# The mlp of an RWKV/NSA block: loads and weight sums moved ahead at its two seams, 512-column products in the up projection, and an accumulator in seven separate PSUM banks

## The chip, the cores and the metric

One core of one Trainium2 chip runs the whole program. The metric is device time in microseconds (us), the median of three runs. TensorE (PE) multiplies, VectorE (DVE), ScalarE (ACT) and GpSimd (POOL) do the elementwise work, SyncE (SP) issues most of the transfers.

## The reference, cut to what matters

One block for 512 tokens of width 2048; the change touches the lines from `h` on. `D_FF` is 8192.

```python
mixed = jax.nn.sigmoid(gate_a) * (y_a @ w_out_rwkv[l]) + jax.nn.sigmoid(gate_b) * (y_b @ w_out_nsa[l])
h = h + mixed @ w_o[l]
hn = rmsnorm(h, norm_mlp[l])
h = h + jnp.square(jax.nn.relu(hn @ mlp_w_up[l])) @ mlp_w_down[l]
...
return rmsnorm(h, norm_final)
```

## The kernel before

Matrices stay transposed: 128 features on the partitions, the T = 512 tokens along a row. To keep float32 accuracy every factor is split into a high and a low part (type fp32r), and a product is three matmuls into one PSUM accumulator: hi·x_hi, hi·x_lo, lo·x_hi.

**Jobs.** The projections `w_on`, `w_o` and `w_down` are jobs of one queue (`add_job`, L74). A job is one block of 128 output rows: 16 k-tiles, three matmuls each (L100 to L102), in an accumulator `acc`. Weights come in pieces of four k-tiles (`split`, L60: load `wraw` on SP's queue, ACT casts `whi`, DVE subtracts for `wlo`), prefetched two pieces ahead. A job's `evac` reads the accumulator once it is complete.

**The w_o jobs** (`o_evac`, L144) make `h`, store it to `hd` in device memory, and add up its squares on POOL (two operations of each block, L1159 and L1161, for the norm's sum `ssq`). ACT scales `h` into `q`, and of each pair of blocks `factors` (L172) makes one tile `hx`: seven linear combinations of four quarters (two feature blocks by two token halves of H = 256), each in a high and a low part. hx0 to hx5 are made while the jobs run, hx6 and hx7 at the head of `mlp_up`.

**The up projection** (`mlp_up`, L1203) computes 32 column blocks j with a Strassen–Winograd scheme: seven products of quarter size in place of eight, each over two halves of the k-tiles (kh = 0, 1). A product in one half is four k-tiles by three matmuls of 256 columns, so a half is 84 matmuls and a block j 168. `prep` (L1215) makes the weights of a half one half ahead: SP loads 1 MB `raw`, DVE and POOL make the sums s1 and s2 (half of each on either engine), ACT casts `h3` (three plain weights) and `hs` (two sums, twice), DVE subtracts for the low parts `l3` (L1225) and `ls` (L1233). `hs` and `ls` have two buffers each: one for s1 and one for s2, so those of the next half must wait until the products of this half have read them. The accumulator of a block has eight slots of 256 columns in four banks; two accumulators alternate over j, so that the evacuation of one block (`evac`, L1253: one ACT copy, four DVE additions, relu and square on ACT, a store to `ud`) lies beside the products of the next block.

The norm's scale is computed on the way: `rms` and `bcast` are called inside the first half's products, and its square `rb` multiplies the down projection's sum at the end, since relu and square let a positive factor through.

**The down projection** (`mlp_down`, L1296) has four quarters q of 16 jobs. `hidden(j)` (L1305) loads `u` from `ud` and splits it into `xs`. The last quarter runs in two token halves; each of its evacuations multiplies by `rb`, adds `h` (loaded again as `hl`, L1359) and adds up squares for the final norm.

**What sets the order.** PE and POOL run in the order in which the code is written (`manual_schedule`). DVE, ACT and SP are ordered by the compiler's scheduler within what the data allow; buffers (`bufs=`) decide when a tile may be written again. SP's instructions issue in order: one that waits holds up those behind it.

## Time and profile before

| | |
|---|---|
| median of three runs | 3146.84 us (3144.91 to 3146.86) |
| the profiled execution | 3148.25 us, span of its trace 3146.5 us, mean clock 0.99 |
| DVE busy, share of the span | 58% |
| ACT busy, share of the span | 38% |
| POOL busy, share of the span | 20% |

The up projection runs from 1723.7 to about 2372.9 us of the span, the down projection from there to the end. A row of the timeline gives an instruction's start, its duration, engine, line and operation, and in brackets the idle time ahead of it with what ended that. A row of a stretch gives the busy time of each engine, the granted clock of PE (1.00 is the full 2.4 GHz), the share of time in which the DMA engines moved data, and GB/s.

### The profile page before, as it was taken

To read this page: it belongs to the slowest core of one execution; us is meant where nothing else is said; L and a number is where in the kernel's file an instruction comes from. 1 tells how busy PE (TensorE), PEld (TensorE's weight loads), DVE (VectorE), ACT (ScalarE), POOL (GpSimd) and SP (SyncE) were. 2 spreads that over 40 slices of the span, in tenths; PEclk is the share of its full clock that TensorE was granted. 3 is DMA by queue.
4 is the path that set the end of the run, shared out by engine and by line. 5 is a ranking of instruction groups with operands and counts; after the bars stand their busy time and mean duration, and the time that the engine had idled before them with its cause. 6 is when DMAs were issued, how large, how long until landed. Compare 5 with 4: busy or idle time off the path is not lost.

```text
span 3146.5 us, 49636 instructions
## 1 busy us (share of the span) xinstructions
PE 3051.5 (97%) x19296; PEld 2589.6 (82%) x19296; DVE 1824.0 (58%) x3220; ACT 1181.7 (38%) x1999; POOL 644.1 (20%) x673
## 2 busy tenths in 40 slices
PE   9999999999999999999998999999997999999997
PEld 7777777777777878777887999999996888888987
DVE  7855665575553457774455677777774233332665
ACT  4322332233222345554333444444443232222443
POOL 2312222222220000001222333333330000000244
PEclk9999999999999999999999999999998999999999
DMA  4222222222224422125544333333335242342565
GB/s 162 81 87 76 79 79 75 71 81 85 78 77 145 133 92 65 62 90 189 167 147 131 127 132 131 133 131 132 132 118 193 95 148 94 105 137 94 166 198 178
DMA packets 167901, 369.29 MB, mean 117 GB/s; under 512 B 18928, under 2 KB 28656, under 8 KB 159472
## 3 DMA queue, kind: packets, MB, share of 16 engines
q1 hardware_dynamic: 156384, 339.28, 33.1%
q10 hardware_dynamic: 10640, 24.73, 2.1%
q8 instruction: 151, 2.47, 0.3%
q0 software_dynamic: 640, 2.10, 0.2%
q14 instruction: 86, 0.70, 0.1%
HBM read 322.06 MB, written 41.94 MB: 116 GB/s over the span
## 4 chain that ended last, share of the span: by engine, by line
PE 61%; DVE 2%; DMA 1%; ACT 1%; issue 1%; POOL 0%; SPq 0%; DVEq 0%; ACTq 0%; POOLq 0%
PE acc L1247 20%; PE acc L100 12%; PE acc L102 12%; PE acc L101 12%; PE po L1036 1%; PE sc L1003 1%; PE pt L1025 1%; DMA wraw<-w_down 1%; DMA u<-ud 1%; DVE wlo L68 0%; PE sc L947 0%; ACT whi L67 0%; DVE hx L1186 0%; PE po L982 0%; DVE kst L921 0%
## 5 line engine op out<-in xcount | busy, mean ns | idle before, releaser
L68 DVE TENSOR_TENSOR wlo<-wraw,whi 128x512 fp32r<-128x512 f32 x752 | 541.5, 723 | 590.1 <-ACT whi L67 585.2
L67 ACT CAST whi<-wraw 128x512 fp32r<-128x512 f32 x752 | 465.0, 619 | 1090.7 <-PE acc L101 978.5
L100 PE MATMUL acc<-xn,whi 128*128 128x512 f32 x1472 | 611.5, 415 | 1.3 <-DVE th L380 1.3
L102 PE MATMUL acc<-xn,wlo 128*128 128x512 f32 x1472 | 578.4, 393 | 0.0
L101 PE MATMUL acc<-xn,whi 128*128 128x512 f32 x1472 | 577.4, 392 | 0.0
L100 PE MATMUL acc<-xs,whi 128*128 128x512 f32 (+1 forms) x1280 | 450.4, 352 | 21.2 <-ACT xs L925 16.2
L102 PE MATMUL acc<-xs,wlo 128*128 128x512 f32 (+1 forms) x1280 | 449.8, 351 | 1.9 <-DVE wlo L68 1.9
L101 PE MATMUL acc<-xs,whi 128*128 128x512 f32 (+1 forms) x1280 | 449.5, 351 | 2.0 <-DVE xs L926 2.0
L1247 PE MATMUL acc<-hx,hs 128*128 128x256 f32 x2048 | 365.8, 281 | 0.0
L100 PEld LDWEIGHTS acc<-xn,whi 128*128 128x128 f32 x1472 | 278.3, 189 | 60.4 <-issue 6.5
L102 PEld LDWEIGHTS acc<-xn,wlo 128*128 128x128 f32 x1472 | 277.5, 189 | 61.4
L101 PEld LDWEIGHTS acc<-xn,whi 128*128 128x128 f32 x1472 | 278.7, 189 | 46.1
L1247 PEld LDWEIGHTS acc<-hx,hs 128*128 128x128 f32 x2048 | 315.2, 189 | 0.0
L100 PEld LDWEIGHTS acc<-xs,whi 128*128 128x128 f32 x1280 | 241.5, 189 | 58.8 <-ACT xs L925 17.3
L1247 PE MATMUL acc<-hx,ls 128*128 128x256 f32 x1024 | 287.6, 281 | 0.0
L1247 PE MATMUL acc<-hx,h 128*128 128x256 f32 x1536 | 276.9, 282 | 4.7 <-ACT h L1224 4.7
L101 PEld LDWEIGHTS acc<-xs,whi 128*128 128x128 f32 x1280 | 241.5, 189 | 38.8 <-DVE xs L926 3.9
L102 PEld LDWEIGHTS acc<-xs,wlo 128*128 128x128 f32 x1280 | 241.6, 189 | 38.5 <-DVE wlo L68 3.4
L1233 DVE TENSOR_TENSOR ls<-s,hs 128x1024 fp32r<-128x1024 f32 x128 | 181.2, 1416 | 109.1 <-ACT hs L1232 109.1
L1247 PEld LDWEIGHTS acc<-hx,h 128*128 128x128 f32 x1536 | 237.0, 190 | 5.2 <-ACT h L1224 5.2
L1247 PE MATMUL acc<-hx,l 128*128 128x256 f32 x768 | 216.5, 282 | 5.2 <-DVE l L1225 5.2
L1247 PEld LDWEIGHTS acc<-hx,ls 128*128 128x128 f32 x1024 | 193.3, 189 | 0.0
(351 smaller groups left out, 4217.3 us busy)
## 6 DMA issues: line engine op xcount, KB each, us to landing
wraw<-w_down SPq DMA_DIRECT2D x320, 256.0 KB, 3.2
raw<-w_up SPq DMA_DIRECT2D x64, 1024.0 KB, 5.0
wraw<-w_gate SPq DMA_DIRECT2D x128, 256.0 KB, 3.0
wraw<-w_rkv SPq DMA_DIRECT2D x96, 256.0 KB, 3.1
wraw<-w_o SPq DMA_DIRECT2D x64, 256.0 KB, 3.2
ud<-e ACTq DMA_DIRECT2D x32, 512.0 KB, 3.7
u<-ud SPq DMA_DIRECT2D x32, 512.0 KB, 5.3
thd<-th SPq DMA_DIRECT2D x32, 256.0 KB, 3.5
```

The costliest lines, as they stand in the source:

```text
L67: nc.scalar.copy(hi, raw)
L68: lo_eng.tensor_tensor(lo, raw, hi.bitcast(F32), OP.subtract)
L100: nc.tensor.matmul(ps, hi[:, j], xh, start=k == 0, stop=False)
L101: nc.tensor.matmul(ps, hi[:, j], xl, start=False, stop=False)
L102: nc.tensor.matmul(ps, lo[:, j], xh, start=False, stop=last)
L1003: nc.tensor.matmul(ps[:, 0:n], q, self.kst[h][:, x, br, 0:n], start=x == 0, stop=x == 1)
L1025: nc.tensor.transpose(pt[:, b], s[:, 128 * b:128 * b + 128], self.ident)
L1036: nc.tensor.matmul(self.o[j][64 * h:64 * h + 64, 128 * i:128 * i + 128], self.vn[:, b, v0:v0 + 64], pT[h][:, b], start=False, stop=i == 3 ...
L1233: nc.vector.tensor_tensor(l, s, h.bitcast(F32), OP.subtract)
L1247: nc.tensor.matmul(o, w[wi][part][:, 128 * i:128 * i + 128], x[:, xi, xp], start=kh == 0 and i == 0 and m == 0 and slot in opens, stop=kh ...
```

## The change

1. **The last four w_o jobs are cut in two**: first k-tiles 0 to 11 of all four, then the last four k-tiles of each, in four accumulators that stay open (`box`, `close`). Their evacuations are called in `mlp_up`, behind the first `prep`, with the second `prep` behind them. `hx6` and `hx7` lie in a pool `px` that opens where the pool `po` closed.
2. **The norm's sum of squares** goes straight into `self.rb`, and its scale is computed in the first quarter of the down projection.
3. **From j = 2 on the products are "wide"**: hi·[x_hi | x_lo] is one matmul of 512 columns, which leaves the two partial sums side by side in one bank, and lo·x_hi (256 columns) is added to the first of them. Seven products take seven banks: four in accumulator A, three in B, and there is one of each, for all j. The evacuation comes in two parts. `evac_a` reads A after the fourth product of the second half, `evac_b` reads B after the seventh.
4. **At the seam to the down projection** its first loads, the job list and two pieces of weights are written ahead of the last block's `evac_b`.
5. **At the end** the factor `rb` and the load of `hl` go to the third quarter (q = 2), and the squares of the last quarter go from POOL to ACT.

```diff
@@ step / add_job
-            ps = self.acc_pool.tile([128, T], F32, name="acc", bufs=2)
+            if job[4]:
+                ps = job[4].pop()
+            else:
+                ps = self.acc_pool.tile([128, T], F32, name="acc", bufs=self.accs)[:, 0:job[1][0][0].shape[-1]]
...
+            if not close:
+                box.append(ps)
+            else:
+                evac(ps, ld) if load else evac(ps)
@@ mix
-        for m in range(KC):
+        for m in range(KC - 4):
             self.add_job(a["w_o"][m], self.xs, *self.o_evac(m))
-        self.drain(KC)
+        boxes = [[] for m in range(4)]
+        for c, ks in enumerate((slice(0, 12), slice(12, 16))):
+            for m in range(4):
+                evac, load = self.o_evac(KC - 4 + m)
+                self.add_job(a["w_o"][KC - 4 + m][:, ks], self.xs[ks], lambda *v, evac=evac: self.last.append((evac, v)),
+                             load if c else None, boxes[m], close=c == 1)
+        self.drain(KC + 4)
@@ o_evac
-            sq = self.ssq if m == 0 else p.tile([128, T], F32, name="sq", bufs=1)
+            sq = self.rb if m == 0 else p.tile([128, T], F32, name="sq", bufs=1)
@@ mlp_up
+        banks = ((0, 0, 2), (1, 5, 4), (2, 3, 3), (3, 4, 5), (4, 1, 0), (5, 6, 1), (6, 2, 6))
+        def wide(A, B, w, kh, ns):
+            for b, wi, xi in banks[ns]:
+                o = (A if b < 4 else B)[:, b % 4]
+                for i in range(4):
+                    x = self.hx[4 * kh + i]
+                    ws = slice(128 * i, 128 * i + 128)
+                    nc.tensor.matmul(o, w[wi][0][:, ws], x[:, xi].rearrange("p a t -> p (a t)"),
+                                     start=kh == 0 and i == 0, stop=kh == 1 and i == 3, skip_group_check=True)
+                    nc.tensor.matmul(o[:, 0:H], w[wi][1][:, ws], x[:, xi, 0], start=False,
+                                     stop=kh == 1 and i == 3, skip_group_check=True)
+        def evac_a(A):
+            nc.scalar.copy(e[:, 0:7:2], A[:, :, H:T])
+            nc.vector.tensor_tensor(e[:, 0:7:2], A[:, :, 0:H], e[:, 0:7:2], OP.add)
+            nc.vector.tensor_tensor(e[:, 2], e[:, 0], e[:, 2], OP.add)
+            nc.vector.tensor_tensor(e[:, 3:7:3], b2(e[:, 2]), e[:, 4:7:2], OP.add)
+            nc.vector.tensor_tensor(f[:, 3], e[:, 6], e[:, 4], OP.add)
+        def evac_b(j, B, e, f):
+            nc.vector.tensor_tensor(e[:, 0:7:3], B[:, 0:3, 0:H], e[:, 0:7:3], OP.add)
+            nc.vector.tensor_tensor(f[:, 0:3], B[:, 0:3, H:T], e[:, 0:7:3], OP.add)
+            store(j, e[:, 0:4], f)
...
+            wide(*accs, w, kh, slice(0, 4))
+            ef = evac_a(accs[0]) if kh else None
+            wide(*accs, w, kh, slice(4, 7))
+            if kh and j < NU - 1:
+                evac_b(j, accs[1], *ef)
@@ mlp_down
+            for j in range(3):
+                hidden(j)
+            x0 = [None] * KC
+            for m in range(KC):
+                self.add_job(a["w_down"][0, m], x0, lambda ps, m=m: down_evac(0, m)(ps))
+            self.prefetch(2)
+            last_up()
...
+                    if q == 2:
+                        t = p.tile([128, T], F32, name="hl", bufs=2)
+                        nc.sync.dma_start(t, self.hd[m])
+                        nc.vector.tensor_tensor(A[m], A[m], self.rb, OP.mult)
+                        nc.vector.tensor_tensor(A[m], A[m], t, OP.add)
+                    if q == 0 and m == 4:
+                        self.defer(4, rms)
...
-                    nc.vector.tensor_tensor(t, ps, t, OP.add)
-                    nc.vector.tensor_tensor(t, t, self.rb[:, ts], OP.mult)
-                    (nc.vector if m == KC - 1 else nc.gpsimd).tensor_tensor(t, t, hl, OP.add)
+                    u = p.tile([128, T // 2], F32, name="pr", bufs=2)
+                    nc.vector.tensor_tensor(u, ps, self.rb[:, ts], OP.mult)
+                    nc.vector.tensor_tensor(t, u, t, OP.add)
```

How the instructions stand, in three places. A number behind a name tells one tile from the next of that name.

DVE in the middle of the up projection, before, from the low part of the next half's first sums to the low part of its plain weights (`acc7` is a block's accumulator, `e` its evacuation tile):

```order
L1233 TENSOR_TENSOR ls_18770<-s_18759,hs_18769 128x1024 [waits PE_49,Activation_49]
L1220 TENSOR_TENSOR s_18872<-raw_18870 128x512 [waits DVE_49]
L1233 TENSOR_TENSOR ls_18774<-s_18760,hs_18773 128x1024 [waits PE_49,Activation_49]
L1257 TENSOR_TENSOR e_18861<-acc7_18672,e_18861 128x2x256 [waits DMAHW4_49,Activation_49]
L1226 TENSOR_TENSOR s_18873<-s_18872,raw_18870 128x512 [waits DVE_49]
L1258 TENSOR_TENSOR e_18861<-acc7_18672,e_18861 128x256 [waits DVE_49]
L1259 TENSOR_TENSOR e_18861<-acc7_18672,e_18861 128x2x256 [waits DVE_49]
L1260 TENSOR_TENSOR e_18861<-acc7_18672,e_18861 128x512 [waits DVE_49]
L1225 TENSOR_TENSOR l3_18982<-raw_18975,h3_18981 128x1536 [waits DMAHW0_49,PE_49,Activation_49]
```

The same stretch now, from the same operation to the end of the block's evacuation (`acc7_19067` is A, `acc7_19068` is B):

```order
L1249 TENSOR_TENSOR ls_19138<-s_19127,hs_19137 128x1024 [waits PE_49,Activation_49]
L1305 TENSOR_TENSOR e_19177<-acc7_19067,e_19177 128x4x256 [waits Activation_49]
L1236 TENSOR_TENSOR s_19215<-raw_19213 128x512 [waits DMAHW2_49,DVE_49]
L1249 TENSOR_TENSOR ls_19142<-s_19128,hs_19141 128x1024 [waits PE_49,Activation_49]
L1306 TENSOR_TENSOR e_19177<-e_19177 128x256 [waits DVE_49]
L1242 TENSOR_TENSOR s_19216<-s_19215,raw_19213 128x512 [waits DVE_49]
L1307 TENSOR_TENSOR e_19177<-e_19177 128x2x256 [waits DVE_49]
L1241 TENSOR_TENSOR l3_19220<-raw_19213,h3_19219 128x1536 [waits PE_49,Activation_49]
L1308 TENSOR_TENSOR f_19178<-e_19177 128x256 [waits DMAHW0_49,DVE_49]
L1312 TENSOR_TENSOR e_19177<-acc7_19068,e_19177 128x3x256 [waits DVE_49]
L1313 TENSOR_TENSOR f_19178<-acc7_19068,e_19177 128x768 [waits DVE_49]
```

Before, the four additions of an evacuation stood between two low parts and read an accumulator that PE needed again only a block later; now six stand there, the two that read B are the last of the row, and `l3` stands ahead of them.

PE where one block follows the other, before:

```order
L1247 MATMUL acc7_19326<-hx6_17047,ls_19323 128x256
L1247 MATMUL acc7_19326<-hx7_17048,hs_19322 128x256 x2
L1247 MATMUL acc7_19326<-hx7_17048,ls_19323 128x256
L1247 MATMUL acc7_19544<-hx0_15657,h3_19417 128x256 [waits PE_49]
L1247 MATMUL acc7_19544<-hx0_15657,h3_19417 128x256
L1247 MATMUL acc7_19544<-hx0_15657,l3_19418 128x256
```

PE now, where the products of the next block pass from A to B in its first half:

```order
L1298 MATMUL acc7_19067<-hx2_15659,ls_18972 128x256
L1296 MATMUL acc7_19067<-hx3_15660,hs_18971 128x512
L1298 MATMUL acc7_19067<-hx3_15660,ls_18972 128x256
L1296 MATMUL acc7_19068<-hx0_15657,h3_18965 128x512 [waits DVE_49,PE_49]
L1298 MATMUL acc7_19068<-hx0_15657,l3_18966 128x256
```

The first matmul of a block waited for PE alone; the first into B now waits for DVE, whose operation there is the last row of the piece above, of the block ahead.

DVE at the seam from the up to the down projection, before (L68 is the low part of a down weight, L926 that of `xs`):

```order
L1257 TENSOR_TENSOR e_24073<-acc7_23904,e_24073 128x2x256 [waits DMAHW4_49,Activation_49]
L1258 TENSOR_TENSOR e_24073<-acc7_23904,e_24073 128x256 [waits DVE_49]
L1259 TENSOR_TENSOR e_24073<-acc7_23904,e_24073 128x2x256 [waits DVE_49]
L1260 TENSOR_TENSOR e_24073<-acc7_23904,e_24073 128x512 [waits DVE_49]
L68 TENSOR_TENSOR wlo_24157<-wraw_24155,whi_24156 128x512 [waits DMAHW6_49,Activation_49]
L68 TENSOR_TENSOR wlo_24163<-wraw_24161,whi_24162 128x512 [waits DMAHW7_49,Activation_49]
L68 TENSOR_TENSOR wlo_24169<-wraw_24167,whi_24168 128x512 [waits DMAHW0_49,Activation_49]
L926 TENSOR_TENSOR xs_24098<-u_24096,xs_24098 128x1024 [waits DMAHW6_49,Activation_49]
```

And now:

```order
L68 TENSOR_TENSOR wlo_22540<-wraw_22538,whi_22539 128x512 [waits DMAHW6_49,DVE_49,Activation_49]
L68 TENSOR_TENSOR wlo_22546<-wraw_22544,whi_22545 128x512 [waits DMAHW7_49,DVE_49,Activation_49]
L1305 TENSOR_TENSOR e_22477<-acc7_22387,e_22477 128x4x256 [waits Activation_49]
L68 TENSOR_TENSOR wlo_22602<-wraw_22600,whi_22601 128x512 [waits DMAHW0_49,Activation_49]
L1306 TENSOR_TENSOR e_22477<-e_22477 128x256 [waits DVE_49]
L1307 TENSOR_TENSOR e_22477<-e_22477 128x2x256 [waits DVE_49]
L1308 TENSOR_TENSOR f_22478<-e_22477 128x256 [waits DMAHW4_49,DVE_49]
L1312 TENSOR_TENSOR e_22477<-acc7_22388,e_22477 128x3x256 [waits DVE_49,PE_49]
L1313 TENSOR_TENSOR f_22478<-acc7_22388,e_22477 128x768 [waits DVE_49]
L933 TENSOR_TENSOR xs_22525<-u_22523,xs_22525 128x1024 [waits DMAHW5_49,Activation_49]
```

The three low parts of down weights stood behind the last block's evacuation and now stand ahead of it or inside its first part; on SP's queue seven weight loads are followed by the loads of `u`, as before.

## Rows read from the trace of the kernel before

**Rows 1.** The page, busy time of each engine and share of the span.

```profile
PE 3051.5 (97%) x19296; PEld 2589.6 (82%) x19296; DVE 1824.0 (58%) x3220; ACT 1181.7 (38%) x1999; POOL 644.1 (20%) x673
```

**Rows 2.** PE's waits from 1600 us on: us in total, times, longest.

```profile
PE rb L164 <- POOL rsy L149: 5.8, 2, 4.4
PE acc L1247 <- DVE l L1225: 5.2, 1, 5.2
...
PE acc L1247 <- ACT h L1224: 4.7, 1, 4.7
```

**Rows 3.** Timeline of DVE, 2000 to 2041 us, one block of the up projection.

```profile
2000.23 0.41 DVE L1258 TENSOR_TENSOR e<-acc,e 128x256 f32<-128x256 f32 x1
...
2019.43 0.68 DVE L1226 TENSOR_TENSOR s<-s,raw 128x512 f32<-128x512 f32 x1
2020.03 0.41 DVE L1258 TENSOR_TENSOR e<-acc,e 128x256 f32<-128x256 f32 x1
...
2021.20 0.69 DVE L1260 TENSOR_TENSOR e<-acc,e 128x512 f32<-128x512 f32 x1
2022.18 1.76 DVE L1225 TENSOR_TENSOR l<-raw,h 128x1536 fp32r<-128x1536 f32 x1 [0.29 <-ACT h L1224]
2025.17 1.23 DVE L1233 TENSOR_TENSOR ls<-s,hs 128x1024 fp32r<-128x1024 f32 x1 [1.23 <-ACT hs L1232]
```

**Rows 4.** Timeline of ACT, the same block.

```profile
2006.55 1.05 ACT L1232 CAST hs<-s 128x1024 fp32r<-128x1024 f32 x1 [1.21 <-PE acc L1247]
```

**Rows 5.** Timeline of POOL in three places of the up projection and its head.

```profile
1719.88 1.35 POOL L1159 TENSOR_TENSOR sq<-h 128x512 f32<-128x512 f32 x1 [8.15 <-DVE h L1156]
...
1728.10 3.79 POOL L1227 TENSOR_TENSOR s<-raw,s 128x512 f32<-128x512 f32 x1 [3.23 <-DVE s L1226]
1789.35 1.79 POOL L1221 TENSOR_TENSOR s<-raw 128x512 f32<-128x512 f32 x1 [4.86 <-DVE ls L1233]
2010.42 1.29 POOL L1227 TENSOR_TENSOR s<-raw,s 128x512 f32<-128x512 f32 x1 [1.95 <-DVE s L1226]
```

**Rows 6.** Timeline of DVE beside two of them.

```profile
1729.55 1.21 DVE L1233 TENSOR_TENSOR ls<-s,hs 128x1024 fp32r<-128x1024 f32 x1
...
1789.91 2.31 DVE L1233 TENSOR_TENSOR ls<-s,hs 128x1024 fp32r<-128x1024 f32 x1
```

**Rows 7.** Timeline of PE in the down projection, two matmuls 48 matmuls apart.

```profile
2500.14 0.40 PE L100 MATMUL acc<-xs,whi 128*128 128x512 f32 x1
...
2511.34 0.40 PE L100 MATMUL acc<-xs,whi 128*128 128x512 f32 x1
```

**Rows 8.** Stretches: length, busy PE, PEld, DVE, ACT, POOL; PE's clock, DMA share, GB/s.

```profile
867.00:870.00 3.00, 0.50 (x3) 0.08 (x2) 0.45 (x1) 0.73 (x2) 1.74 (x7) 1.00 0.25 87
870.00:873.00 3.00, 3.00 (x12) 2.47 (x13) 2.52 (x5) 1.55 (x3) 0.00 (x0) 0.73 0.16 53
873.00:876.00 3.00, 3.00 (x11) 2.36 (x10) 1.33 (x4) 0.00 (x0) 0.00 (x0) 0.70 0.24 84
3031.00:3034.00 3.00, 1.54 (x14) 1.34 (x13) 0.72 (x2) 0.60 (x3) 1.63 (x6) 1.00 0.25 85
```

**Rows 9.** Timeline of PE, the first matmul of the down projection.

```profile
2388.25 0.79 PE L100 MATMUL acc<-xs,whi 128*128 128x512 f32 x1 [15.34 <-ACT xs L925]
```

**Rows 10.** Timelines of DVE and SP at that seam.

```profile
2379.11 0.69 DVE L68 TENSOR_TENSOR wlo<-wraw,whi 128x512 fp32r<-128x512 f32 x1 [0.77 <-ACT whi L67]
...
2380.21 1.55 SPq L1307 DMA_DIRECT2D u<-ud  x3
```

**Rows 11.** A stretch of the last quarter, columns as in rows 8.

```profile
3020.00:3120.00 100.00, 90.08 (x727) 86.76 (x726) 60.03 (x103) 43.36 (x76) 47.04 (x59) 1.00 0.66 197
```

**Rows 12.** The chain that ended last, inside that stretch: start, us, what.

```profile
3036.75 3.07 POOL h L1366
...
3039.84 0.33 SPq L1359
...
3040.27 4.26 DMA wraw<-w_down
```

More of the change, by code (lines that the diff above doesn't have):

```diff
@@ L69, in split, with add_job @@
         return hi, lo
-    def add_job(self, src, xs, evac, load=None):
-        self.jobs.append((src, xs, evac, load))
+    def add_job(self, src, xs, evac, load=None, box=None, close=True):
+        self.jobs.append((src, xs, evac, load, box, close))
         for h in range(len(xs) // WK):
@@ L88, in step @@
             job = self.jobs.popleft()
[L89 to L91 removed]
+            if job[4]:
+                ps = job[4].pop()
+            else:
+                ps = self.acc_pool.tile([128, T], F32, name="acc", bufs=self.accs)[:, 0:job[1][0][0].shape[-1]]
+            self.cur = [job, ps, 0, job[3] and job[3](), job[4] is None or job[5] is False]
+        (src, xs, evac, load, box, close), ps, k, ld, opens = self.cur
         if k % WK == 0:
@@ L99, in step @@
         last = k == len(xs) - 1
-        nc.tensor.matmul(ps, hi[:, j], xh, start=k == 0, stop=False)
+        nc.tensor.matmul(ps, hi[:, j], xh, start=opens and k == 0, stop=False)
         nc.tensor.matmul(ps, hi[:, j], xl, start=False, stop=False)
-        nc.tensor.matmul(ps, lo[:, j], xh, start=False, stop=last)
+        nc.tensor.matmul(ps, lo[:, j], xh, start=False, stop=close and last)
         self.cur[2] += 1
@@ L1092, in stage3 @@
             self.ps3 = ctx.enter_context(ExitStack())
-            self.acc_pool = self.ps3.enter_context(tc.tile_pool(name="ps3", bufs=1, space=PSUM))
+            self.acc_pool = self.ps3.enter_context(tc.tile_pool(name="ps3", bufs=1, space=PSUM, side="right"))
+            self.accs = 4
             self.mix()
             self.project_out()
-            self.mlp_up()
-            self.mlp_down(out)
+            self.mlp_down(out, self.mlp_up())
+            self.tops.close()
     def mix(self):
@@ L1195, in project_out @@
             self.hx.append(t)
-        self.late = []
+        self.late, self.last = [], []
         self.pop = ExitStack()
-        self.po = self.pop.enter_context(tc.tile_pool(name="po", bufs=1, reuse_waits="tile"))
-        self.ssq = self.po.tile([128, T], F32, name="ssq")
+        self.pq = self.pop.enter_context(tc.tile_pool(name="pq", bufs=1, reuse_waits="tile"))
+        self.pop2 = ExitStack()
+        self.po = self.pop2.enter_context(tc.tile_pool(name="po", bufs=1, reuse_waits="tile"))
         self.drain()
@@ L1239, in mlp_up, with products @@
         opens = {3, 1, 5, 6}
-        def products(acc, w, kh, hook):
-            for n, (slot, wi, xi) in enumerate(prods):
+        def products(acc, w, kh):
+            for slot, wi, xi in prods:
                 o = acc[:, slot]
@@ L1260, in evac @@
[L1260 to L1272 removed]
+            nc.vector.tensor_tensor(e[:, 2], acc[:, 2], e[:, 1], OP.add)
@@ L1276, in mlp_up, with mlp_down @@
         ahead = [prep(*order[0])]
-        for q, t in zip(self.late, self.hx[6:]):
-            self.factors(self.po, t, q)
+        for evac_o, v in self.last:
+            evac_o(*v)
+        ahead.append(prep(*order[1]))
+        self.pop2.close()
+        px = right(st, "px")
+        for k in range(6, 8):
+            t = px.tile([128, 7, 2, H], F32R, name=f"hx{k}")
+            self.hx.append(t)
+            self.factors(self.pq, t, self.late[k - 6])
+        self.ps3.close()
+        psa[1] = self.psb.enter_context(tc.tile_pool(name="psb", bufs=1, space=PSUM, side="right"))
         for n, (j, kh) in enumerate(order):
-            if n + 1 < len(order):
+            if n and n + 1 < len(order):
                 ahead.append(prep(*order[n + 1]))
-            if kh == 0:
-                if j == 1:
-                    psa[1] = st.enter_context(tc.tile_pool(name="psb", bufs=1, space=PSUM, side="right"))
-                accs[j] = psa[j % 2].tile([128, 8, H], F32, name="acc7")
-            products(accs[j], ahead.pop(0), kh, {1: rms, 5: bcast} if n == 0 else {})
-            if n == 0:
-                self.ps3.close()
-                self.pop.close()
-                pe = st.enter_context(tc.tile_pool(name="pe", bufs=1, reuse_waits="tile"))
-            if kh:
-                evac(j, accs.pop(j))
+            w = ahead.pop(0)
+            if j < 2:
+                if kh == 0:
+                    accs[j] = psa[j].tile([128, 8, H], F32, name="acc7")
+                products(accs[j], w, kh)
+                if kh:
+                    evac(j, accs.pop(j))
+                if n == 3:
+                    self.pop.close()
+                continue
+            if kh == 0:
+                accs = [t.tile([128, 4, T], F32, name="acc7") for t in psa]
+            wide(*accs, w, kh, slice(0, 4))
[3 more added lines that the diff above has]
+                evac_b(j, accs[1], *ef)
         st.close()
         self.hxp.close()
-    def mlp_down(self, out):
+        return lambda: evac_b(NU - 1, accs[1], *ef)
+    def mlp_down(self, out, last_up):
         nc, tc, a = self.nc, self.tc, self.a
+        self.accs = 2
         with ExitStack() as ctx:
@@ L1373, in evac @@
                         final(2 * m - 3, halves[0], nc.gpsimd, rf[:, halves[0]])
-                return evac, load
+                return evac
             for q in range(3):
-                for m in range(KC):
+                for m in range(KC if q else 0):
                     self.add_job(a["w_down"][q, m], [xs[16 * q + k] for k in range(KC)], down_evac(q, m))
```

90 lines of the change are left out of this document (45 added, 45 removed).

## The prediction

> **What bounds the kernel now.** I read the shares of busy time first. PE works 97% of the span and no other engine comes near [rows 1], so time falls where PE waits or where its matmuls take less, and it grows with every new wait of PE. Next come PE's waits from 1600 us on. At the head of the up projection PE waits 4.7 us for the cast of its first weights, 5.2 us for their low parts and 4.4 us (the longest of two) for the norm's scale [rows 2], and at the seam to the down projection 15.3 us for the first `xs` [rows 9]. Between the two seams, for 32 blocks, these views show no wait worth a row. There I read the timeline of DVE, because a block's period is what 29 repetitions will multiply: the same addition stands at 2000.23 and at 2020.03 [rows 3], so a block takes 19.80 us, and PE fills it with 168 matmuls of 256 columns, 117.9 ns each. DVE has time to spare there, but in the kernel before nothing that PE needs hangs on the end of its row. That is what the change alters.
>
> **Parts 1 and 2, the head of the up projection: 0 us, between −9 and +5.** The three waits make 14.3 us. With the last four jobs cut, the first weights are loaded and cast while PE still has work, and the scale is no longer asked for here. That would give most of 14 us. Against it: the four late evacuations put eight POOL operations of 1.35 us [rows 5] one behind the other, 10.8 us, behind the last w_o products. The tile hx6 lies where the pool of these operations was, so ACT's cast for it waits for the last of them, and on ACT the `hs` cast of the next half is queued behind that. PE has 84 matmuls of the first half (9.9 us) and parts of the second to cover it. Working forward from the end of the jobs I get a new wait of 4 to 10 us in the second half, and the raw load is issued only some 1.5 to 2 us earlier than before, since it stands behind two stores of `h` on SP's queue. The new wait eats the gain: 0. If it were hidden, −9; if hx7 and the next sums come late too, +5.
>
> **Part 3, the matmuls: −4 us, between −20 and 0.** A block had 168 matmuls of 256 columns; it has 56 of 512 and 56 of 256. A 512-column matmul takes (2511.34 − 2500.14)/48 = 233.3 ns in the down projection [rows 7], against 235.8 for two of 256. So 56 × (233.3 + 117.9) = 19.67 us a block, 0.13 less than 19.80, and 30 blocks have it: −4. The upper bound is no saving at all; the lower bound pays what a 256-column matmul has above its columns (117.9 − 106.7 at 2.4 GHz, 11.2 ns) only once in the merged one: 213.3 + 11.2 = 224.5 against 235.8, 56 times, is 0.63 a block, 19 in all, rounded to 20. I take the measured pitch, whose row is of the same shape.
>
> **Part 3, the evacuation: +65 us, between +33 and +75.** There was an accumulator in reserve; now A and B are used again by the next block. PE's first matmul into B, in the next block's first half, waits for the last DVE operation of this evacuation, which the order piece shows at the end of eleven. Count from the moment at which the fourth product of the second half is done (A complete, t = 0). PE still has three products for B, then four for A of the next block, before it needs B: seven products of 4 × (233.3 + 117.9) = 1.405 us, so it arrives at t = 9.83.
>
> DVE's row starts with the low part `ls` of the next half's sums. Its tile is free only when the fourth product is done, and ACT must cast first (1.05 us, released by PE [rows 4]), so DVE starts at about t = 1.2. From rows 3: `ls` 1.23 (1024 elements), the addition that reads all four banks of A 1.23 (as long as `ls`, since 512 elements take 0.69 from PSUM and 0.68 from SBUF), s1 0.68, `ls` 1.23, 0.41 (256), s2 0.68, 0.69 (512), `l3` 1.76, 0.41, and the two that read B, 768 elements each and so 0.96 (midway between 0.69 and 1.23). Sum 10.24. Independent neighbours overlap by 0.08 (2019.43 + 0.68 against 2020.03), dependent ones leave about 0.04 (1.17 from 2020.03 to 2021.20 for 0.41 + 0.69 and two junctions): eight and two make −0.56, so 9.68. DVE is done at 10.9 and PE goes on at about 11.0, 1.15 us late in each block.
>
> POOL adds to this. Its half of s2 (1.29 us alone [rows 5]) is issued when DVE's half is done, beside the 512-element addition; `l3`, which reads two tiles in SBUF, comes next on DVE while POOL is still in it. Before, three additions that read PSUM stood there. When DVE and POOL meet with operands in SBUF, one takes the time of both: at 1789 us POOL started first, and `ls` beside it took 2.31 instead of 1.23 [rows 6], 1.08 more; at 1728 POOL started 1.45 us ahead of `ls`, and yet `ls` took 1.21 and POOL 3.79 [rows 5, 6]. If POOL goes first, the stall is 1.15 + 1.08 = 2.23 us. The blocks j = 3 to 31 wait for the one before: 29 × 2.23 = 65. Without the meeting 29 × 1.15 = 33; with a little more of it (2.6) 75. I take 65, because POOL is here well inside its operation when DVE comes, as at 1789.
>
> The page "SBUF — State Buffer" of the Trainium skill, section "Who interferes with whom", states that a tensor_tensor of DVE with two SBUF inputs contends with a GpSimd instruction that reads SBUF, that whoever issues first has the shared ports for its whole instruction, and that issue order, not the operation's shape, decides who blocks. By that rule alone the sum would be 65 us; by the row at 1728.10, which speaks against it, 33 us. The trace here shows both.
>
> **Part 4, the seam to the down projection: −8 us, between −4 and −12.** The last matmul of the up projection ends at 2388.25 − 15.34 = 2372.91 [rows 9]; call it T. The loads of `u` are issued at 2380.21 [rows 10], T + 7.3, behind the seventh weight load, which waits for the buffer that the third `wlo` frees. This `wlo` started at 2379.11 [rows 10]: DVE had the whole evacuation ahead of it. Now it stands behind the first part alone. That part starts at A's end, 4.2 us ahead of T, so `wlo` ends at T − 4.2 + 0.15 + 1.05 + 1.23 + 0.69 = T − 1.1, and the loads are issued 8.4 us earlier. The rest of the seam keeps its length, load, cast and subtraction, so the first matmul comes at about T + 6.9, not T + 15.3. I take 8 for a part of it that may end on another wait; −4 if the buffers of `u` or ACT (which now has relu and square behind A) come later, −12 if the loads overlap better.
>
> **Part 5, the last quarter: −7 us, between −10 and 0.** From 3020 to 3120 us PE is busy 90.08 of 100 [rows 11], so 9.9 are idle, 1.46 of them in the norm's stretch [rows 8], which stays. The chain names what holds the rest: weight loads of 4.26 us, issued late on SP behind the `hl` loads, and these behind POOL's addition of `h`, 3.07 us [rows 12]. The `hl` loads and that addition leave the last quarter. In the third quarter they lie beside PE's work: two DVE operations and a load for each job, 16 times, at 11.2 us a job (48 × 233.3 ns). If that cover failed, each job there would add up to 1.4 us. The norm's scale, moved to the first quarter, costs some ten small matmuls, about 1 us, in the 7. I take 7 of 8.4.
>
> **Sum.** 3148.25 (the profiled execution, of which 3146.5 is span) − 4 + 65 + 0 − 8 − 7 = 3194 us. The profiled execution is 1.4 us above the median of the runs, so 3193 us for the median. Break-even lies where the stall is 19/29 = 0.66 us a block.
>
> **Rivals.**
> - *The clock falls as well.* After 2.5 us of idle PE in 3, the granted clock stood at 0.73 and 0.70 for the next two stretches of 3 us [rows 8], which costs (0.27 + 0.30) × 3 = 1.7 us. If each stall of about 2 us did this, 29 × 1.7 = 49 more: 3242. Against it: 1.46 idle of 3 us at 3031 left the clock at 1.00 [rows 8]. The stalls lie between these two.
> - *DVE keeps the ports*, as at 1728. Stall 1.15, +33: 3161.
> - *The evacuation keeps up, and the kernel gets faster.* This is the other side. My chain is a sum of eleven operations and a start; if it is 0.5 us shorter (10.4 in place of 10.9), the stall falls under 0.66, and if it is 1.15 shorter nothing waits: 3146.84 − 4 − 8 − 7 = 3128, and down to 3119 if the head gains its 9. For it: DVE is busy 58% of the span, and the operations that feed the next half's weights could in principle run elsewhere in the period. Against it: the same addition takes 0.41 in both blocks [rows 3], each duration has its row, and the order on DVE is fixed.
> - *The merged product does not do what it says.* If a 512-column matmul costs as much as two of 256, the 4 us are gone: 3197. This is inside the forecast's own range.
>
> **How the numbers follow.** Forecast, POOL between and the clock steady: 0.52, 3193, its own range 3175 to 3205. Clock falls: 0.17, up to 3242. DVE keeps the ports: 0.18, about 3150 to 3172. Keeps up: 0.13, 3115 to 3140. A measurement of this kernel can tell about 0.2%, 6.3 us, from no change. Faster by more: 0.13, the last case. Within: 0.07, a third of the case of 3161, where part 3's matmuls or the head gain more. Slower: 0.80. The range leaves out the faster case and a little of both ends: 3150 to 3240.
>
> **What would show it.** In the profile after, PE should wait once a block, at the first 512-column matmul into B of a first half, for DVE's last addition, 2.2 us on average; about 1.15 and no long `l3` would mean that DVE keeps the ports; no such row, that the evacuation keeps up. `l3` or the 256-element addition behind it should last some 1.08 us longer than 1.76 or 0.41. The period should be 19.7 us plus the stall. A granted clock under 1.00 in the up projection is the second rival. At the head a wait for `hs` or hx6 in the second half in place of the three; at the seam a wait of about 7 us for `xs`; in the last quarter PE busy over 97 of 100. The forecast is wrong if the period stays under 20.4 us.

## The result and the profile after

The changed kernel takes 3232.34 us (median of four runs, 3229.49 to 3235.83), before 3146.77: a ratio of 1.0274 (95% interval 1.0256 to 1.0292), 85.6 us slower. The forecast was slower, 3193 us, with a range from 3150 to 3240. Its profiled execution has a span of 3227.7 us at a mean clock of 0.98.

The page still shows a busy PE; what is new stands in PE's waits from 1600 us on (us in total, times, longest), in place of [rows 2]:

```profile
PE 3088.7 (96%) x17616; PEld 2539.5 (79%) x17616; DVE 1904.1 (59%) x3312; ACT 1218.7 (38%) x2031; POOL 617.7 (19%) x613
```
```profile
PE acc L1296 <- DVE f L1313: 64.6, 29, 2.3
PE acc L104 <- ACT xs L932: 4.7, 1, 4.7
PE acc L1263 <- ACT hs L1248: 3.5, 1, 3.5
PE acc L1263 <- ACT h L1240: 3.0, 1, 3.0
...
PE acc L1298 <- DVE ls L1249: 2.4, 1, 2.4
PE acc L1263 <- DVE ls L1249: 2.1, 1, 2.1
PE acc L1263 <- DVE l L1241: 2.1, 1, 2.1
```

29 waits for L1313, the last addition of `evac_b`, make 64.6 us. The seam to the down projection has 4.7 in place of 15.3 [rows 9]. At the head four waits (L1263), 10.7 us together, stand where three made 14.3. One more of 2.4 us, for `ls` (L1298), stands in the first half with wide products.

One block on DVE, with POOL's operation beside it and PE's first matmul into B (timelines of the three engines):

```profile
2050.56 1.23 DVE L1249 TENSOR_TENSOR ls<-s,hs 128x1024 fp32r<-128x1024 f32 x1 [3.42 <-ACT hs L1248]
2051.70 1.22 DVE L1305 TENSOR_TENSOR e<-acc,e 128x1024 f32<-128x1024 f32 x1
...
2055.71 0.68 DVE L1307 TENSOR_TENSOR e<-e 128x512 f32<-128x512 f32 x1
2056.31 2.84 DVE L1241 TENSOR_TENSOR l<-raw,h 128x1536 fp32r<-128x1536 f32 x1
2059.07 0.41 DVE L1308 TENSOR_TENSOR f<-e 128x256 f32<-128x256 f32 x1
2059.52 0.96 DVE L1312 TENSOR_TENSOR e<-acc,e 128x768 f32<-128x768 f32 x1
2060.51 0.96 DVE L1313 TENSOR_TENSOR f<-acc,e 128x768 f32<-128x768 f32 x1
```
```profile
2055.92 1.61 POOL L1243 TENSOR_TENSOR s<-raw,s 128x512 f32<-128x512 f32 x1 [2.76 <-DVE s L1242]
```
```profile
2037.88 0.47 PE L1296 MATMUL acc<-hx,h 128*128 128x512 f32 x1 [2.23 <-DVE f L1313]
...
2061.61 0.47 PE L1296 MATMUL acc<-hx,h 128*128 128x512 f32 x1 [2.23 <-DVE f L1313]
```

This is the chain of the forecast, row for row: POOL starts at 2055.92, `l3` comes at 2056.31 and takes 2.84 in place of 1.76 [rows 3], and PE waits 2.23 us, the value forecast.

But this block now takes 23.73 us (2061.61 − 2037.88), and 19.7 + 2.2 is 21.9. Most of the rest is the clock. Stretches of the changed kernel (columns as in [rows 8]):

```profile
1780.00:2360.00 580.00, 526.52 (x2775) 452.02 (x2774) 401.75 (x392) 251.25 (x223) 178.18 (x100) 0.94 0.32 114
2059.00:2062.00 3.00, 0.77 (x5) 0.43 (x4) 2.93 (x5) 1.54 (x2) 0.00 (x0) 1.00 0.51 161
2062.39:2065.39 3.00, 3.00 (x12) 2.51 (x11) 0.90 (x2) 1.23 (x2) 1.79 (x1) 0.52 0.62 257
```

Behind a wait the granted clock falls to nearly its lower level (0.52 in a stretch of 3 us); over 580 us of the up projection it is 0.94, where the kernel before had 1.00. Not every wait has such a fall behind it. Of the 28 periods from one of these waits to the next, 24 are 23.6 to 23.8 us long and four are 22.2. Here is one of the four, from PE's timeline, and the stretches of this period and of the next, a long one:

```profile
1803.59 0.47 PE L1296 MATMUL acc<-hx,h 128*128 128x512 f32 x1 [2.23 <-DVE f L1313]
...
1825.80 0.48 PE L1296 MATMUL acc<-hx,h 128*128 128x512 f32 x1 [2.23 <-DVE f L1313]
```
```profile
1803.70:1825.70 22.00, 19.87 (x112) 17.04 (x112) 16.04 (x17) 10.00 (x10) 7.37 (x4) 1.00 0.31 114
1825.90:1849.40 23.50, 21.43 (x112) 18.34 (x112) 16.09 (x17) 9.98 (x9) 7.49 (x4) 0.93 0.30 108
```

So a fall costs about 1.5 us (23.73 − 22.21). The remaining 0.3 us of a period (22.21 − 19.7 − 2.23) is lost beside the wait with the clock at 1.00.

From the first to the last matmul of the up projection it is 759.0 us, before 649.2: 109.8 more. The seam takes 10.7 less. The second token half of the last quarter, with the end behind it, takes 108.1 in place of 121.1.

### The profile page after: what moved, and what is told of

Read it like the earlier page. It is cut to its first block, busy times and chain, and to the rows that moved or that the text cites. A ratio compares the mean times of both kernels' runs of the same rounds, so it can differ in the third digit from the quotient of the medians.

```text
span 3227.7 us, 46415 instructions
## 1 busy us (share of the span) xinstructions
PE 3088.7 (96%) x17616; PEld 2539.5 (79%) x17616; DVE 1904.1 (59%) x3312; ACT 1218.7 (38%) x2031; POOL 617.7 (19%) x613
## 4 chain that ended last, share of the span: by engine, by line
PE 52%; DVE 11%; issue 2%; ACT 1%; POOL 1%; DMA 0%; DVEq 0%; ACTq 0%; SPq 0%; POOLq 0%
PE acc L104 13%; PE acc L105 12%; PE acc L106 12%; PE acc L1296 7%; PE acc L1298 3%; DVE l L1241 2%; DVE ls L1249 2%; PE po L1043 1%; PE sc L1010 1%; PE pt L1032 1%; ACT hs L1248 1%; DVE e L1312 1%; DVE f L1313 1%; DVE s L1236 1%; DVE e L1305 1%
## 5 line engine op out<-in xcount | busy, mean ns | idle before, releaser
L68 DVE TENSOR_TENSOR wlo<-wraw,whi 128x512 fp32r<-128x512 f32 x752 | 532.2, 709 | 567.6 <-ACT whi L67 559.1
L1296 PE MATMUL acc<-hx,hs 128*128 128x512 f32 x960 | 365.3, 416 | 0.3 <-ACT hs L1248 0.3
L1296 PE MATMUL acc<-hx,h 128*128 128x512 f32 x720 | 276.2, 418 | 64.6 <-DVE f L1313 64.6
L1249 DVE TENSOR_TENSOR ls<-s,hs 128x1024 fp32r<-128x1024 f32 x128 | 161.7, 1263 | 207.7 <-ACT hs L1248 207.7
L1298 PE MATMUL acc<-hx,ls 128*128 128x256 f32 x960 | 280.1, 292 | 2.4 <-DVE ls L1249 2.4
L1248 ACT CAST hs<-s 128x1024 fp32r<-128x1024 f32 x128 | 134.2, 1049 | 343.3 <-PE acc L1296 335.3
L1296 PEld LDWEIGHTS acc<-hx,hs 128*128 128x128 f32 x960 | 192.6, 201 | 48.6 <-ACT hs L1248 0.7
L1296 PEld LDWEIGHTS acc<-hx,h 128*128 128x128 f32 x720 | 142.7, 198 | 107.0 <-issue 73.3
L1298 PE MATMUL acc<-hx,l 128*128 128x256 f32 x720 | 210.9, 293 | 0.0
```

Of the source, the lines that this page charges most:

```text
L68: lo_eng.tensor_tensor(lo, raw, hi.bitcast(F32), OP.subtract)
L1248: nc.scalar.copy(h, s)
L1249: nc.vector.tensor_tensor(l, s, h.bitcast(F32), OP.subtract)
L1296: nc.tensor.matmul(o, w[wi][0][:, ws], x[:, xi].rearrange("p a t -> p (a t)"), start=kh == 0 and i == 0, stop=kh == 1 and i == 3, skip_gro ...
L1298: nc.tensor.matmul(o[:, 0:H], w[wi][1][:, ws], x[:, xi, 0], start=False, stop=kh == 1 and i == 3, skip_group_check=True)
```

## Experiments

Each run was compared with runs of the kernel before on the same chip; their medians lay at 3145.7 to 3147.6 us.

### Which part costs, which part gains

The seams alone, part 3 undone:

```diff
-                accs = [t.tile([128, 4, T], F32, name="acc7") for t in psa]
-            wide(*accs, w, kh, slice(0, 4))
-            ef = evac_a(accs[0]) if kh else None
-            wide(*accs, w, kh, slice(4, 7))
-            if kh and j < NU - 1:
-                evac_b(j, accs[1], *ef)
+                acc = psa[j % 2].tile([128, 8, H], F32, name="acc7")
+            products(acc, w, kh)
+            if kh and j < NU - 1:
+                evac(j, acc)
```

> The changed kernel with part 3 undone: products of 256 columns and two alternating accumulators for all 32 blocks; parts 1, 2, 4 and 5 as they are. Theory (the wait for B and the clock behind it are the whole loss, and the rest of the change gains what the two traces show at the seams: 10.7 us less at the seam to the down projection, 12.9 less behind the last quarter's first half, 1.8 less at the head, and perhaps some us of waits in the first four halves): 3114 to 3122 us, and no wait of PE for the evacuation in the up projection. Rival (the seams gain only what was forecast, 15 us, and the rest of the trace's difference is something that depends on the new products): 3130 to 3134.

3125.96 us, ratio 0.9936 (0.9922 to 0.9951): 19.7 us faster than before, between the two expectations. No wait for the evacuation. The seam has 4.9 us and the end 110.1, close to the changed kernel's 4.7 and 108.1; the head gains little (waits of 4.6, 1.8, 3.1 and 2.1).

Part 3 alone, in the kernel before:

```diff
-            products(accs[j], ahead.pop(0), kh, {1: rms, 5: bcast} if n == 0 else {})
+            w = ahead.pop(0)
+            if j < 2:
+                products(accs[j], w, kh, {1: rms, 5: bcast} if n == 0 else {})
+            else:
+                wide(*accs[j], w, kh, slice(0, 4))
+                ef = evac_a(accs[j][0]) if kh else None
+                wide(*accs[j], w, kh, slice(4, 7))
...
+            elif kh:
+                evac_b(j, accs.pop(j)[1], *ef)
```

> The kernel before with part 3 alone: 512-column products, seven banks, evacuation in two parts; head, seams and last quarter as before. Theory (part 3 costs the same by itself: 29 waits of 2.23 us and a clock that falls behind nearly all of them, some 110 us): 3250 to 3265. Rival (the loss needs the changed seams or the buffers' new places): under 3235.

3251.91 us, ratio 1.0336 (1.0320 to 1.0351): 106.2 us slower, with 29 waits of 2.4 us for the last addition and a clock of 0.94. −19.7 + 106.2 = 86.5 against 85.6 for the whole: the two add up. The whole loss is part 3's.

### Is it the place in DVE's row?

ACT takes B out, so that PE no longer waits for DVE's last additions:

```diff
+            if j < NU - 1:
+                g = pg.tile([128, 3, T], F32, name="g", bufs=1)
+                nc.scalar.copy(g, B[:, 0:3])
+                B = g
             nc.vector.tensor_tensor(e[:, 0:7:3], B[:, 0:3, 0:H], e[:, 0:7:3], OP.add)
```

> The changed kernel, in which ACT copies the three banks of B into SBUF as soon as they are complete (1536 elements, about 1.5 us, behind the cast of h3) and DVE's last two additions read the copy: the same work and one copy more, but PE no longer waits for the end of DVE's row. Theory (the wait on the last addition is the cause): B is free some 7.3 us after A is complete and PE comes at 9.8, so no wait and no fall of the clock in the up projection, 3110 to 3122 us. Rival (DVE is too busy in any case: the low parts of the next half come late in place of the addition): waits of 0.5 to 1.2 us a block for ls, 3130 to 3155.

3151.54 us. The waits for B are gone and the clock is 1.00 again, but a new wait is there, as the rival said (PE's waits):

```profile
PE acc L1298 <- DVE ls L1249: 23.0, 30, 2.4
```

The timeline of ACT shows where it comes from:

```profile
2054.25 1.06 ACT L1270 ACTIVATE e<-f 128x1024 f32<-128x1024 f32 x1 [1.17 <-DVE f L1317]
2055.34 1.06 ACT L1271 ACTIVATE f<-e 128x1024 f32<-128x1024 f32 x1
2056.31 1.04 ACT L1248 CAST hs<-s 128x1024 fp32r<-128x1024 f32 x1
```

The cast for the next sums stands on ACT behind the relu, and the relu waits for DVE's last addition, which comes at the end of the same row. With the relu put behind that cast:

```diff
                 ahead.append(prep(*order[n + 1]))
+                if late:
+                    with tc.issue_after(cast[order[n + 1]].ins):
+                        store(*late.pop())
```

(`cast` keeps the last cast of each half, `late` what `evac_b` would have given to `store`.)

> The run in which ACT copies B, with ACT's order altered: the relu of a block is issued behind the cast of the next but one half's second sums. Theory (there the 30 waits of 0.77 us for ls came from ACT's queue: the relu waited for DVE's last addition, and the cast behind it was ready 1.2 us earlier): the waits go, 3124 to 3132 us. Rival (DVE itself is late): waits stay at 0.5 us or more, over 3140.

3141.43 us, 10 less, with 14.3 us of waits for `ls` left (29): 0.7 us a block fell to 0.4. A good third was ACT's queue; the rest is DVE, as the rival had it (the second low part takes 2.32 us there, as in the next run).

The order on DVE alone, with every operation, tile and buffer as in the changed kernel:

```diff
-            nc.vector.tensor_tensor(l3, raw[:, 0:3], h3.bitcast(F32), OP.subtract)
-            nc.vector.tensor_tensor(s2[:, 0], s1[:, 0], raw[:, 0], OP.subtract)
+            with tc.issue_after(fb[j - 1].ins) if kh and j - 1 in fb else ExitStack():
+                nc.vector.tensor_tensor(s2[:, 0], s1[:, 0], raw[:, 0], OP.subtract)
+                nc.vector.tensor_tensor(l3, raw[:, 0:3], h3.bitcast(F32), OP.subtract)
```

(`fb` keeps each block's last addition.)

> The changed kernel with nothing but DVE's order altered: for every second half the first part of s2 and l3 are issued behind the block's last addition, which reads B, and no longer ahead of it. All operations, tiles and buffers are as in the changed kernel. Theory (the place in DVE's row is the cause, not the work): the row up to the last addition is 2.4 us shorter by these two and loses the meeting of l3 and POOL, so it ends some 8.5 us after A is complete, before PE comes at 9.8: no wait for B, no fall of the clock, 3120 to 3128 us (the seams' gain of the seams run, and 2.6 us less for the matmuls). Rival (the work that is put behind comes late in its turn, as the low parts did when ACT copied B): waits of 0.2 to 0.8 us a block for ls or l3, 3130 to 3150.

3149.92 us: 82 us less than the changed kernel by order alone, no wait for B, clock 1.00. But the rival was right about the rest, 29 waits for `ls` (21.2 us), and DVE's timeline shows both low parts of the next sums beside POOL:

```profile
2053.64 2.32 DVE L1252 TENSOR_TENSOR ls<-s,hs 128x1024 fp32r<-128x1024 f32 x1
2055.99 0.69 DVE L1238 TENSOR_TENSOR s<-raw 128x512 f32<-128x512 f32 x1
2056.60 2.32 DVE L1252 TENSOR_TENSOR ls<-s,hs 128x1024 fp32r<-128x1024 f32 x1
```

So, with the head's improvement from below added, POOL's half of s1 was made to wait until the second of these is done:

```diff
-            nc.gpsimd.tensor_tensor(s1[:, 1], raw[:, 0], raw[:, 3], OP.subtract)
+            sub = nc.gpsimd.tensor_tensor(s1[:, 1], raw[:, 0], raw[:, 3], OP.subtract)
+            if j > 2 and not kh:
+                tc.add_manual_dep(sub.ins, low[-1].ins.name, ...)
```

> DVE's order and the head altered, and POOL's half of s1 for each first half made to wait for the low parts of the sums ahead of it, so that it no longer meets them on DVE. Theory (in the order run the waits of 0.7 us for ls came from two low parts that took 2.32 in place of 1.22 beside POOL): the second of them takes 1.22 again, the 29 waits go, and with them some 28 us less than the order-and-head run: 3116 to 3122 us, the same as the seams-and-head run within 4 us, since the merged products alone are worth 1.5 to 3 us. Rival (the row is late anyway, by the first of the two low parts): waits of 0.3 us or more stay, over 3126.

3121.93 us (ratio 0.9920, 0.9905 to 0.9934), 24.2 below the run with order and head alone. That second low part takes 1.22:

```profile
2042.67 2.32 DVE L1255 TENSOR_TENSOR ls<-s,hs 128x1024 fp32r<-128x1024 f32 x1
2045.02 0.69 DVE L1238 TENSOR_TENSOR s<-raw 128x512 f32<-128x512 f32 x1
2045.63 1.22 DVE L1255 TENSOR_TENSOR ls<-s,hs 128x1024 fp32r<-128x1024 f32 x1
```

and the repeated wait is gone (a single wait of 2.4 us for `ls` is left there). The wait for B and the wait for the next sums were one problem: a row of DVE operations, run in order, with little slack between two results that PE waits for.

### The meeting with POOL, and the clock

POOL's half of s2 given to DVE (`nc.gpsimd` to `nc.vector` in that line):

> The changed kernel with POOL's half of s2 given to DVE, which takes 0.69 us for it between the last addition of the first part and the two that read B. No meeting of POOL and l3: l3 back at 1.76 from 2.84. Theory on the row: the wait falls from 2.23 to 1.15 + 0.61 = 1.76 us, 29 times, 13.6 us less. On the clock: if a wait of 1.76 still lets it fall as often, 3217 to 3221 us; if the clock stays at full speed behind the shorter wait, some 42 us more are gone, 3172 to 3180. Rival to the meeting (l3 was long for another reason): l3 stays at 2.8 and the wait grows to 2.8, over 3240.

3171.28 us. `l3` is back at 1.74 us, so the meeting had made it long. The wait is 46.4 / 29 = 1.60 us, and the clock stays: 61 us less, of which the shorter wait explains 18.

```profile
2058.28 1.74 DVE L1241 TENSOR_TENSOR l<-raw,h 128x1536 fp32r<-128x1536 f32 x1
```

The stretches of this run, the second and third at one wait and just behind it:

```profile
1780.00:2360.00 580.00, 538.36 (x3024) 464.02 (x3024) 436.42 (x484) 274.97 (x243) 83.46 (x54) 1.00 0.34 123
2060.00:2063.00 3.00, 1.40 (x9) 0.98 (x7) 2.97 (x6) 1.19 (x2) 0.00 (x0) 1.00 0.36 57
2063.50:2066.50 3.00, 3.00 (x19) 2.62 (x18) 1.14 (x2) 2.08 (x3) 1.80 (x1) 1.00 0.75 313
```

That could have been the wait's length or the meeting itself. So the wait was made long again without a meeting, by making that addition on DVE twice, and once and a half:

```diff
             nc.vector.tensor_tensor(s2[:, 1], raw[:, 1], s2[:, 0], OP.subtract)
+            nc.vector.tensor_tensor(s2[:, 1], raw[:, 1], s2[:, 0], OP.subtract)
```

> The run in which DVE makes all of s2, with that addition (0.69 us) made twice on DVE each time. POOL and l3 still do not meet. The wait for B grows by some 0.55 us, from 1.60 to about 2.15, close to the 2.23 of the changed kernel. Theory (the clock falls because of the length of the wait): it falls behind most of the 29 waits again, and the time is 3171 + 16 + some 40 = 3222 to 3232 us. Rival (the clock fell for something that comes with the meeting of POOL and DVE, not for the wait): it stays, 3185 to 3190.

> The same with half of that addition made again (256 elements, 0.41 us): the wait should be about 1.9 us. If the clock holds as behind 1.60: 3177 to 3183 us. If it falls as behind 2.23: 3215 to 3225; between these, a part of the 29 blocks shows a fall.

3228.08 and 3211.98 us, with waits of 61.2 / 29 = 2.11 and 53.5 / 29 = 1.84 us. From 1.60 to 1.84 us the waits grow by 7 us in all and the time by 40.7. In the stretch from 1780 to 2360 us the clock of the second is 0.95:

```profile
1780.00:2360.00 580.00, 533.79 (x2839) 457.90 (x2838) 428.09 (x505) 258.42 (x228) 79.04 (x51) 0.95 0.33 116
```

So the clock falls without the meeting too, and what was changed to bring that about is the length of the wait. Length alone does not settle each case: in the second run 20 of the 28 periods are long and 8 short, behind waits of nearly one length (last section).

### The head

The first raw load put ahead of the stores of `h` on SP, in the seams run:

```diff
-            x = self.po.tile([128, T], F32, name="ld", bufs=2)
+            x = self.po.tile([128, T], F32, name="ld", bufs=4)
...
-        for evac_o, v in self.last:
-            evac_o(*v)
+        with tc.issue_after(self.ld.ins):
+            for evac_o, v in self.last:
+                evac_o(*v)
```

(`self.ld` is the raw load.)

> The seams run (products of 256 columns) with SP's order at the head altered: the first raw load is issued ahead of the stores of h and no longer stands behind them and the last two loads of x, for which there are four buffers in place of two. Theory (the head gained nothing because the load was queued behind these): the raw load is issued some 5 to 7 us earlier, the waits of 4.6 and 1.8 us for h3 and l3 go, POOL's eight operations end some 6 us earlier, and the waits of 3.1 and 2.1 for hs and ls go with them: 10 us less than the seams run, 3113 to 3119. Rival (the load waits for memory that PE's last matmuls still read): no change, 3123 to 3129.

3117.94 us, ratio 0.9908 (0.9893 to 0.9924). The load is issued at 1706.02 us of the span, 12.9 us before the last w_o matmul ends, against 3.7 in the changed kernel; the wait for `h3` is gone, and two waits for `l3` (0.2 and 0.7) are left of the other. The waits for `hs` and `ls` stay (3.9, 2.1), so that half of the expectation failed, and the gain is 8 us. The same with the order on DVE (both diffs together, in the changed kernel):

> DVE's order altered as in the order run and SP's at the head as in the head run, together. Both theories: 3110 to 3117 us, below every other kernel here. If the head's load waits for memory: as the order run alone. If the order run has waits for ls: that many us above.

3146.15 us, 4 below the order run; the waits for `ls` stay.

Last, in the run with seams and head, POOL's first four late operations ahead of its parts of the first weight sums:

```diff
-        ahead = [prep(*order[0])]
-        with tc.issue_after(self.ld.ins):
-            for evac_o, v in self.last:
-                evac_o(*v)
+        raw0 = fetch(*order[0])
+        with tc.issue_after(self.ld.ins):
+            for evac_o, v in self.last[:2]:
+                evac_o(*v)
+        ahead = [prep(*order[0], raw0)]
+        for evac_o, v in self.last[2:]:
+            evac_o(*v)
```

(`fetch` is `prep`'s raw load.)

> The seams-and-head run with POOL's order at the head altered as well: the squares and sums of the first two late blocks are issued ahead of POOL's parts of the first half's weight sums, in the time in which POOL waited for the first raw load. Theory (the waits of 3.9 and 2.1 us for hs and ls in the second half come from POOL's chain of eight operations, behind which ACT's cast for hx6 waits and the casts of the next sums behind that): the chain ends some 6 to 8 us earlier, both waits go, 6 us less: 3110 to 3114. Rival (something else holds the casts, or the first sums come late in their turn): 3117 or more.

3117.95 us, no gain. The chain on POOL did end earlier, the wait for `hs` went and that for `ls` shrank from 2.1 to 1.6 (in two), but a new one came in their place, 4.1 us for `l3`. The timeline of DVE shows why:

```profile
1715.58 1.52 DVE L1198 TENSOR_TENSOR T<-q 128x256 f32<-128x256 f32 x1
1717.02 1.50 DVE L1199 TENSOR_TENSOR T<-q,T 128x256 f32<-128x256 f32 x1
...
1720.44 2.50 DVE L1245 TENSOR_TENSOR l<-raw,h 128x1536 fp32r<-128x1536 f32 x1
```

Additions of 256 elements take 1.5 us beside POOL's operations for the sum of squares, where they take 0.4 alone, and `l3` stands behind them.

The seams with the head's load first, 3118 us with products of 256 columns, beat both kernels. The wide products with both orders mended (3122 us) are no better, so their merging is worth nothing that these runs can tell.

## Why the prediction was right, and where it was not

| term | forecast | measured |
|---|---|---|
| matmuls | −4 | −2 |
| waits for B | +65 | +64.6 |
| clock | a rival, +49, chance 0.17 | about +40 |
| beside each wait, clock at 1.00 | not counted | +5 to +8 |
| wait for `ls` in the first wide half | not counted | +2.4 |
| head | 0 | −3.6 |
| seam to the down projection | −8 | −10.7 |
| last quarter | −7 | −9 to −11 |

**The direction and the wait: right by its own chain.** 29 waits, 2.23 us each, `l3` at 2.84: the sum over DVE's row came out at the measured value (some of that is luck: by the same sum the run with s2 on DVE should have waited 1.76, and waited 1.60), and the runs showed each link, the order (82 us by order alone) and the meeting with POOL (`l3` at 1.74 without it).

**The step that failed is the clock.** The forecast gave a steady clock 0.52 and its fall 0.17, because 1.46 us of idle in 3 had left it at 1.00 [rows 8]. The measured waits lay above that row, and it was no evidence for them. The price of a fall was near: 1.7 us forecast, 1.5 measured. The 40 are from two sides: 0.06 of some 700 us is 42, and 1.5 us behind 25 of the 29 waits (24 long periods, and a clock of 0.50 behind the last wait, 2462.20 to 2465.20) are 38. The forecast's favoured case had a range of 3175 to 3205, and 3232 lies outside it; the whole range holds it only because it reached nearly to the rival's 3242.

**What the forecast did not count.** A wait of PE costs a little more than its recorded length with the clock at 1.00: 22.21 − 19.72 − 2.23 = 0.26 us here, and 21.50 − 19.72 − 1.60 = 0.18 in the run with s2 on DVE (the waits that end at 2019.97 and 2041.47). Over 29 waits that is 5 to 8 us. The wait of 2.4 us for `ls` is 1.3 in the part-3 run and absent from the seams run; its cause was not looked for. With all rows of the table 3193 becomes 3232 to 3237, against 3232.

**A row was misread**, though not on the side that decided. The rival in which DVE keeps the ports rested on [rows 5, 6] at 1728: POOL ahead of `ls` by 1.45 us and yet the loser. The timeline of the kernel before has, ahead of that `ls`:

```profile
1727.88 1.74 DVE L1225 TENSOR_TENSOR l<-raw,h 128x1536 fp32r<-128x1536 f32 x1
1729.55 1.21 DVE L1233 TENSOR_TENSOR ls<-s,hs 128x1024 fp32r<-128x1024 f32 x1
```

DVE was in `l3` since 1727.88, 0.22 us ahead of POOL, so POOL came second and had to wait for it. The changed kernel shows both orders of arrival: POOL ahead of `l3` above, and here DVE ahead by 0.23 us, where `l3` takes 1.75 and POOL 2.67:

```profile
2045.38 1.75 DVE L1241 TENSOR_TENSOR l<-raw,h 128x1536 fp32r<-128x1536 f32 x1
```
```profile
2045.61 2.67 POOL L1243 TENSOR_TENSOR s<-raw,s 128x512 f32<-128x512 f32 x1 [4.88 <-DVE s L1242]
```

But at 1728 DVE went straight on to `ls`, and POOL, issued 1.45 us ahead of it, waited through that as well. In the order run the same three operations stand at the same spacing, and there POOL came in behind `l3` and made `ls` take 2.32 (above):

```profile
2051.97 1.75 DVE L1245 TENSOR_TENSOR l<-raw,h 128x1536 fp32r<-128x1536 f32 x1
```
```profile
2052.19 2.68 POOL L1246 TENSOR_TENSOR s<-raw,s 128x512 f32<-128x512 f32 x1 [6.05 <-DVE s L1244]
```

At 1789, in the kernel before, a DVE operation with two SBUF inputs also stood just ahead of POOL, which the forecast had read as the first to start, and POOL came in behind it, ahead of `ls`:

```profile
1789.30 0.69 DVE L1220 TENSOR_TENSOR s<-raw 128x512 f32<-128x512 f32 x1
```

So the rule quoted in the forecast, from the Trainium skill's page "SBUF — State Buffer", section "Who interferes with whom", that issue order decides who blocks, agrees with the rows at 1789, 2045, 2052 and 2056 and with POOL's wait for `l3` at 1728, but not with its wait for `ls` there. What let `ls` pass stays open; in the 29 blocks it did not happen.

**The matmuls**: 32 pairs of a 512- and a 256-column matmul take 11.27 us (2045.13 to 2056.40 in the changed kernel), so 56 take 19.72 against 19.80; −4 was −2, inside its range.

**The head** gained 3.6 where 0 was forecast, inside its range and for the reason given, a new wait of 4 to 10 us (5.6) in place of the norm's, and an early load that came only little earlier. What held it was the queue on SP, as the head run showed.

**The seam** was sized at 8 of −4 to −12 and gave 10.7. T is 2482.51 − 4.67 = 2477.84 here. The loads of `u` go out at 2476.96, T − 0.9, as forecast (T − 1.1); but the rest of the seam did not keep its length: the first cast starts 4.5 us behind the issue, and took 6.9 before (2380.21 to 2387.15). The first matmul comes at T + 4.7, not T + 6.9. Why the load lands sooner was not tried.

**The last quarter** was undersized. PE is busy 97.91 of 100 us where [rows 11] had 90.08, as the forecast said it would show:

```profile
3114.00:3214.00 100.00, 97.91 (x826) 97.45 (x824) 64.68 (x113) 54.04 (x101) 20.21 (x33) 1.00 0.62 189
```

All waits for weights left it; the forecast had counted 7 of 8.4 us of them, in one row of the middle. From the second token half to the end, the seams run takes 11.0 us less than the kernel before (110.1 and 121.1), and the changed kernel 9.1 less than the part-3 run, which has the old end (108.1 and 117.2).

## What to carry to other kernels

When an accumulator loses its spare, look for the last operation that reads it on an in-order engine, add up everything queued ahead of it, and ask which of that the next work needs later than the bank: here the order alone was worth 82 us. Look for operations of POOL that start shortly before a DVE operation with two SBUF inputs, and count what the meeting adds (here `l3` took 2.84 us for 1.75). And price a repeated wait of PE twice, once as the wait and once as the clock behind it. A row with a shorter wait at which the clock held says nothing against that, and a single row with one as long says little: four of the waits of 2.23 us left the clock at 1.00.

## What the runs showed of the hardware that was not expected

How sharply the clock follows the length of the wait, and that it does not do so every time. All runs here have 29 waits, one a block, and so 28 periods from wait to wait. A period with a fall of the clock is some 1.5 us longer than one without:

| wait of PE per block, us | mean clock, 1780 to 2360 us | long periods of 28 | time, us |
|---|---|---|---|
| 1.60 | 1.00 | 0 | 3171 |
| 1.84 | 0.95 | 20 | 3212 |
| 2.11 | 0.94 | 24 | 3228 |
| 2.23 | 0.94 | 24 | 3232 |

Three waits in a row from the second line, with a short and a long period between them (21.79 and 23.33 us):

```profile
1825.69 0.47 PE L1297 MATMUL acc<-hx,h 128*128 128x512 f32 x1 [1.82 <-DVE f L1314]
...
1847.48 0.47 PE L1297 MATMUL acc<-hx,h 128*128 128x512 f32 x1 [1.81 <-DVE f L1314]
...
1870.81 0.48 PE L1297 MATMUL acc<-hx,h 128*128 128x512 f32 x1 [1.81 <-DVE f L1314]
```

Between the first two lines of the table 0.24 us more of wait a block cost 1.4 us a block. Where the step lies between them, whether it moves with the work around the wait, and what decides between equal waits, stays open.
